# A two-layer decoder trunk on one core: w_gate and w_up both by seven products in another order, four slots for weight parts and 52 general tiles

## The chip, the cores and the metric

The kernel runs on one core of one Trainium2 chip. The metric is device time in microseconds of one execution, as the median over runs. Its engines are PE (TensorE: matmuls and transposes), PEld (TensorE's weight loads, which run beside PE), DVE (VectorE), ACT (ScalarE), POOL (GpSimd) and SP (SyncE, which issues the DMAs). [...] A difference of 0.2% is about what a measurement of this kernel can tell from no change.

## What is computed

```python
S, D, DEPTH, HID = 512, 1024, 2, 2816          # tokens, model width, layers, FFN width
for layer in range(DEPTH):
    h = h + hybrid_mixer(rmsnorm(h, norm_mix[layer]), w_in[layer], ...)    # attention + Mamba-2, one projection in, one out
    h = h + swiglu(rmsnorm(h, norm_ffn[layer]), w_gate[layer], w_up[layer], w_down[layer])
return rmsnorm(h, final_norm)

def swiglu(h, w_gate, w_up, w_down):            # w_gate, w_up: 1024 x 2816; w_down: 2816 x 1024
    return (silu(h @ w_gate) * (h @ w_up)) @ w_down
```

Everything is float32. The change touches how `h @ w_gate` and `h @ w_up` are made, how much room two pools have, and the first instructions of the program.

## The kernel before

**Layout.** Activations are kept transposed: a tile is 128 features by 512 tokens (2 KB a partition), and `hT` is eight such tiles. A float32 operand is split in two parts, `hi` (the value cast to the faster float32r form) and `lo` (the rest), and each product of two tiles is three matmuls: hi by hi, hi by lo, lo by hi. Of a weight of 128 rows by 128 columns PE loads 128x128 and streams the tokens past it.

**A plan sets the order.** The program first records every operation (`plan.add` with an engine, a cost, its outputs and inputs), each with a due time (`at(...)` and `clock[0]`, which counts PE work). `Plan.schedule` then runs through them as a list scheduler would: each engine takes the ready operation with the smallest due time for which its tiles have room. What comes out is a fixed order for every engine; each engine then works through its own queue strictly in that order and waits where an input or a buffer is missing. SP's loads are taken in the order of their due times alone. Numbers such as the tiles of a pool therefore change the order of everything.

**Pools.** `G(...)` takes a tile of 128x512 from the general pool `g` (`NG` tiles); `whi` and `wlo` hold the two parts of a weight piece of up to eight 128x128 blocks (`NWH` slots each, 4 KB a partition); `raw` holds a weight chunk of 1 MB as it lands (two slots); `big` holds the sums `wsum` (two slots). PSUM has three banks `acc`, two `hold` and three `tr`. `split_w` makes the two parts: ACT casts `raw` to `whi`, DVE subtracts to make `wlo`.

**FFN.** The 22 column tiles of `w_gate` and `w_up` are taken in four parts, `PARTS` = 6, 6, 6, 4. A part takes its tiles in pairs of 256 columns: first `w_gate`, then `w_up`, then SiLU and the product, then the part's rows of `w_down`. Part 0 makes both directly. Parts 1 to 3 make `w_gate` directly: two `block`s of 8 row blocks x 3 = 24 matmuls of 512 columns each, so 48. They make `w_up` by `seven`: the 256 columns, the 1024 rows and the 512 tokens are each cut in two, and the 2x2x2 block product is made with seven products of half size instead of eight (Winograd's form of Strassen). A product is 4 row blocks x 3 = 12 matmuls of 256 tokens, so 84 in all. It needs three weight pieces of eight blocks, called here a (raw columns), b and c (sums of raw blocks), and one of four, d; DVE makes four sums of 128x512 and the parts `wlo`, ACT makes the parts `whi`. The activations' sums (`X`, by `normed`) are made once a layer. In PSUM the products end in `p17`, `p26`, `p45` and `p3`; ACT copies the first, `e`, and five DVE additions make the two column tiles `m` and `o`.

**Start.** SP issues `pmix` (scales), then by turns `hT[k]` and the first weights `raw0[k]` (256 KB each). PE works at once on nine products of `ones`; then, for each k, ACT and DVE split both tiles and PE runs 12 matmuls of 512 columns on them (the first four column tiles of `w_in`). `norm_next.square` squares `hT[k]` on ACT for the first norm.

Of the kernel before, what the change touches and what calls it, by code (L numbers as in the profile page):

```python
# [14 lines left out]
AF = mybir.ActivationFunctionType  # L15
ALU = mybir.AluOpType
# [3 lines left out]
P = 128  # L20
S = 512
# [6 lines left out]
NH = 16  # L28
HID = 2816
NRAW = 2  # L30
NWH = 3
NG = 56
LEAD = 14.0
KTOK = 4
TABLE_COST = 10.0
# [5 lines left out]
E_XW = 'dve'  # L41
RES_G = 6
NEAR_G = 6.0
GATE7 = 0
PARTS = (6, 6, 6, 4)
HH = S // 2
KQ = KD // 2
# [132 lines left out]
class VTile:  # L180


    def __init__(self, pool, shape, dtype, tag, name, space):
        self.pool, self.shape, self.dtype, self.tag, self.name = pool, shape, dtype, tag, name
        self.psum = space
        self.ap = None
        self.writer, self.readers, self.uses = None, [], 0
        self.live = False

    def get(self):  # L190
        if self.ap is None:
# [12 lines left out]
class Plan:  # L204
# [4 lines left out]
    def add(self, eng, dur, outs, ins, fn, prio=None, table=None, lat=0.0):  # L209
        o = Op()  # L210
        o.eng, o.dur, o.lat, o.fn, o.table = eng, dur, lat, fn, table
        o.prio = self.t if prio is None else prio
        o.n, o.users = len(self.ops), []
        deps = set()
        outs = [v.tile for v in outs]
        ins = [v.tile for v in ins if isinstance(v, View)]
        for t in ins:
            assert t.writer is not None, f"{t.name} is read before it is written"
            deps.add(t.writer)
        for t in outs:  # L220
            if t.writer is not None:
                deps.add(t.writer)
            deps.update(t.readers)
        for t in ins:
            t.readers.append(o)
        for t in outs:
            t.writer, t.readers = o, []
        deps.discard(o)
        o.tiles = list({id(t): t for t in outs + ins}.values())
        for t in o.tiles:  # L230
            t.uses += 1
        o.deps = deps
        for d in deps:
            d.users.append(o)
        self.ops.append(o)
        return o
# [107 lines left out]
def hybrid_trunk(  # L344
# [40 lines left out]
    def hold():  # L385
        return new(ps, [P, S], F32, ("hold", 2), "hold", True)
# [39 lines left out]
    def memset(eng, o, val):  # L426
        plan.add(eng, 0.1 + 0.9e-3 * o.free, [o], [], lambda: ENG[eng].memset(R(o), val))

    TABLE = {AF.Exp: "exp", AF.Ln: "ln", AF.Silu: "silu", AF.Sin: "silu"}

    def act(o, a, func, scale=None, bias=None, accum=None):
        ptr = [s for s in (scale, bias) if isinstance(s, View)]
        outs = [o] + ([accum] if accum is not None else [])

        def fn():
            kw = {}
            if scale is not None:
                kw["scale"] = R(scale)
            if bias is not None:
                kw["bias"] = R(bias)  # L440
            if accum is not None:
                kw["accum_out"] = R(accum)
            if func == AF.Copy and not kw:
                nc.scalar.copy(R(o), R(a))  # L444
            else:
                nc.scalar.activation(R(o), R(a), func, **kw)  # L446
        cost = 0.83e-3 * o.free + (0.053 if a.tile.psum else 0.093) + 0.093 * len(ptr)
        plan.add("act", cost, outs, [a] + ptr, fn, table=TABLE.get(func))

    def mms(outs, prods, each, prio=None):  # L450

# [7 lines left out]
                    nc.tensor.matmul(R(p[0]), R(p[1]), R(p[2]), start=p[3], stop=p[4])  # L459
        plan.add("pe", each * len(prods), outs, ins, fn, prio, lat=0.08)  # L460

    def load(o, src, kb):
        plan.add("sp", max(0.47, kb / 351.0), [o], [], lambda: nc.sync.dma_start(R(o), src), lat=2.0)

    def tposes(t, parts, name=None):
        mms([t], parts, 0.108)


    at(-40.0)
    pmix = C([P, 16], "pmix")  # L470
    load(pmix, columns[:, PC_MIX:PC_MIX + 16], 8)
    hT = [C([P, S], f"hT{k}") for k in range(KD)]

    raw0 = []
    for k in range(KD):
        load(hT[k], xT[k * P:(k + 1) * P, :], 256)
        raw0.append(G("w0"))
        load(raw0[k], w_in[0, k * P:(k + 1) * P, XBC_COL + 1024:XBC_COL + 1024 + S], 256)
    at(-35.0)
    ones = C([P, P], "ones")  # L480
    memset("pool", ones, 1.0)

    t = tr()
    mms([t], [(t[:, 0:P], ones, ones, True, True)] * 9, 0.43)
    nhalf = C([P, NT], "nhalf")
    memset("pool", nhalf, -0.5)

# [63 lines left out]
    class Norm:  # L551
# [2 lines left out]
        def __init__(self, n):  # L554
            self.n, self.ss, self.row = n, None, None

        def square(self, tl, eng="dve"):
            s = G("sq")
            act(s, tl, AF.Square)
            if self.ss is None:  # L560
                self.ss = s
            else:
                tt(eng, self.ss, self.ss, s, ALU.add)
# [31 lines left out]
    for k in range(KD):  # L595
        at(-20.0 + k)
        xs_next.append(split_x(hT[k], pmix[:, k:k + 1]))
        wh, wl = split_x(raw0[k], None)
        for j, t in enumerate(first):
            js = slice(j * P, (j + 1) * P)  # L600
            xh, xl = xs_next[k]
            mms([t], [(t, wh[:, js], xh, k == 0, False), (t, wh[:, js], xl, False, False),
                      (t, wl[:, js], xh, False, k == KD - 1)], 0.2165, clock[0])
            clock[0] += 3 * 0.2165
        at(-12.0 + k)
        norm_next.square(hT[k])


    at(-12.0)
# [504 lines left out]
    def seven(ids, X):  # L1114
        raw = whl[ids[0]][0]
        q = [[raw[:, j * KQ:(j + 1) * KQ, i * P:(i + 1) * P] for j in range(2)] for i in range(2)]
        at(clock[0] - LEAD)

        def split(src, nk=KD):
            hi, lo = new(wp, [P, 8, P], F32R, ("whi", NWH), "whi"), new(wp, [P, 8, P], F32R, ("wlo", NWH), "wlo")  # L1120
            copy("act", hi[:, 0:nk, :], src)
            tt("dve", lo[:, 0:nk, :], src, hi[:, 0:nk, :].bitcast(F32), ALU.subtract)
            return hi, lo
        a = split(raw[:, :, 0:P])
        sm = big("wsum").rearrange("p (k c) -> p k c", c=P)
        s = [sm[:, i * KQ:(i + 1) * KQ, :] for i in range(4)]
        tt("dve", s[0], q[1][0], q[1][1], ALU.add)
        tt("dve", s[1], s[0], q[0][0], ALU.add)
        tt("dve", s[2], q[0][0], q[1][0], ALU.add)
        tt("dve", s[3], q[0][1], s[1], ALU.add)  # L1130
        b = split(sm[:, 0:KD, :])
        c = split(sm[:, KD:, :])
        d = split(q[1][1], KQ)
        t1_, t2_ = slice(0, HH), slice(HH, S)

        def prod(o, w, k0, xs, half):
            hi, lo = w
# [12 lines left out]

        def halves(v):
            return v.rearrange("p (u c) -> p u c", u=2)

        b1, b2 = X["b"][0:KQ], X["b"][KQ:]
        p17, p26 = hold(), acc()
        e, m, o = G("e"), G("m"), G("o")
        prod(p17[:, 0:HH], a, 0, b1, t1_)
        copy("act", e[:, 0:HH], p17[:, 0:HH])
        prod(p26[:, 0:HH], a, KQ, b2, t1_)
        prod(p26[:, HH:], b, KQ, X["t12"], t2_)  # L1160
        tt("dve", halves(m), halves(p26), bcast(e[:, 0:HH]), ALU.add)
        p45, p3 = acc(), tr()
        prod(p45[:, HH:], b, 0, X["t12"], t1_)
        prod(p17[:, HH:], c, 0, X["t34"], t1_)
        tt("dve", e[:, HH:], p17[:, HH:], m[:, HH:], ALU.add)
        prod(p3[:, 0:HH], c, KQ, b2, t2_)
        tt("dve", m[:, HH:], m[:, HH:], p3[:, 0:HH], ALU.add)
        tt("dve", m[:, HH:], m[:, HH:], p45[:, HH:], ALU.add)
        prod(p45[:, 0:HH], d, 0, X["t34"], t2_)
        tt("dve", halves(o), halves(p45), bcast(e[:, HH:]), ALU.add)  # L1170
        at(clock[0] - 4.0)
        return m, o

# [100 lines left out]
```

## Time and profile before

| | |
|---|---|
| median of 3 runs | 1323.34 us (1321.87 to 1323.98) |
| the profiled execution | 1324.0 us, of which the span from first to last instruction is 1322.2 us |
| PE busy | 1294.6 us (98%), 6674 matmuls |
| DVE busy | 905.7 us (68%) |
| ACT busy | 653.0 us (49%) |
| POOL busy | 140.2 us (11%) |
| DMA | 115.57 MB, mean 87 GB/s |
| granted clock of TensorE, mean | 0.995 |

Busy is the union of an engine's instructions. A matmul's end is modelled and overlaps the next one's start, so what PE takes for a matmul is read from start to start in the timeline, not from its duration. The same holds for DVE, whose instructions also overlap by some 0.1 us.

### The profile page before, as it was taken

What the parts mean: (1) busy time and instruction counts of PE and PEld (TensorE: products, weight loads), DVE (VectorE), ACT (ScalarE), POOL (GpSimd) and SP (SyncE); (2) the same over time, 40 slices, a digit from 0 to 9 for tenths busy, and PEclk for the clock granted to TensorE, in tenths of its full rate; (3) what the DMA queues carried; (4) which work ended last, traced back from release to release, by engine and by line L of the source; (5) the groups of instructions that cost most, each with busy time, mean ns of one, the idle gap of its engine ahead of it and who ended that gap; (6) DMA issues with size and microseconds to landing.
All of it is one profiled execution on the core that took longest, in us unless ns stands there. A gap on an engine that the chain in (4) does not pass through costs nothing.

```text
span 1322.2 us, 17020 instructions
## 1 busy us (share of the span) xinstructions
PE 1294.6 (98%) x6674; PEld 1067.4 (81%) x6674; DVE 905.7 (68%) x1510; ACT 653.0 (49%) x1029; POOL 140.2 (11%) x109
## 2 busy tenths in 40 slices
PE   8999998999999999999999999999999999999997
PEld 7877776778888888888888777767888889888896
DVE  6987779768746555555779687887786456465464
ACT  7677656656323323323647687466553233243253
POOL 0014455000000000000000234620000000000000
PEclk9999999999999999999999999999999999999999
DMA  7222211123232233233332222111332332322421
GB/s 242 64 64 64 64 65 64 33 80 102 90 112 96 69 123 99 78 112 96 96 98 65 94 66 65 56 40 45 88 112 84 119 96 72 120 96 73 135 96 63
DMA packets 105727, 115.57 MB, mean 87 GB/s; under 512 B 4656, under 2 KB 95024, under 8 KB 105648
## 3 DMA queue, kind: packets, MB, share of 16 engines
q1 hardware_dynamic: 105648, 114.49, 27.4%
q8 instruction: 52, 0.85, 0.3%
q14 instruction: 27, 0.22, 0.1%
HBM read 112.39 MB, written 2.10 MB: 87 GB/s over the span
## 4 chain that ended last, share of the span: by engine, by line
PE 87%; DVE 7%; ACT 2%; POOL 2%; issue 1%; DMA 0%; POOLq 0%; SPq 0%; DVEq 0%; ACTq 0%
PE acc L459 72%; PE hold L459 7%; PE tr L459 6%; PE tr L457 3%; DVE wlo L407 2%; DVE qs L407 1%; POOL xbc L407 1%; DVE xbc L418 1%; POOL qr L407 1%; ACT whi L444 1%; DVE wsum L407 0%; DVE qs L921 0%; POOL qs L407 0%; ACT L446 0%; DVE sa L413 0%
## 5 line engine op out<-in xcount | busy, mean ns | idle before, releaser
L459 PE MATMUL acc<-xh,whi 128*128 128x512 f32 (+1 forms) x1552 | 588.4, 379 | 1.4 <-DVE o L407 0.9
L459 PE MATMUL acc<-xl,whi 128*128 128x512 f32 (+1 forms) x1552 | 579.4, 373 | 0.0
L459 PE MATMUL acc<-xh,wlo 128*128 128x512 f32 (+1 forms) x1536 | 573.3, 373 | 4.2 <-DVE wlo L407 4.2
L444 ACT CAST whi<-raw 128x1024 fp32r<-128x1024 f32 (+3 forms) x248 | 212.4, 859 | 335.2 <-PE acc L459 303.0
L459 PEld LDWEIGHTS acc<-xh,whi 128*128 128x128 f32 x1552 | 293.2, 189 | 55.1 <-issue 5.6
L459 PEld LDWEIGHTS acc<-xh,wlo 128*128 128x128 f32 x1536 | 289.7, 189 | 58.6 <-DVE wlo L407 6.7
L459 PEld LDWEIGHTS acc<-xl,whi 128*128 128x128 f32 x1552 | 293.3, 189 | 47.1 <-issue 0.5
L407 DVE TENSOR_TENSOR wlo<-raw,whi 128x1024 fp32r<-128x1024 f32 (+2 forms) x240 | 246.8, 1030 | 27.6 <-ACT whi L444 27.3
L407 DVE TENSOR_TENSOR hT<-hT,acc 128x512 f32<-128x512 f32 x104 | 71.1, 685 | 103.6 <-PE acc L459 102.9
L407 DVE TENSOR_TENSOR wlo<-wsum,whi 128x1024 fp32r<-128x1024 f32 x32 | 39.0, 1224 | 88.4 <-ACT whi L444 88.4
L573 POOL TENSOR_TENSOR rcol<-var,nhalf 128x4 f32<-128x4 f32 x8 | 8.7, 1089 | 577.2 <-DVE var L413 577.2
L446 ACT ACT_TABLE_LOAD x49 | 62.9, 1283 | 6.6 <-DMA hT<-in_xT_dram 4.1
L444 ACT CAST whi<-wsum 128x1024 fp32r<-128x1024 f32 x32 | 33.5, 1048 | 53.9 <-PE acc L459 46.3
L418 DVE SCALAR_TENSOR_TENSOR xbc<-cu,prm,xbc 128x511 f32<-128x511 f32 (+2 forms) x72 | 58.4, 819 | 0.8
L444 ACT CAST xh<-ga 128x512 fp32r<-128x512 f32 x44 | 27.3, 621 | 54.5 <-DVE ga L407 38.6
L446 ACT ACTIVATE sa<-sa,mx 128x512 f32<-128x512 f32 (+3 forms) x64 | 36.0, 562 | 36.5 <-DVE mx L979 36.2
L1230 POOL TENSOR_TENSOR fr<-fvar,nhalf 128x1 f32<-128x1 f32 x4 | 2.2, 546 | 353.5 <-DVE fvar L413 353.5
L979 DVE CUSTOM_DVE_ANT_0 sa<-tr,cst 128x512 f32<-128x512 f32 (+3 forms) x64 | 30.7, 479 | 10.3 <-PE tr L459 10.2
L459 PE MATMUL hold<-xh,wlo 128*128 128x256 f32 x128 | 36.3, 284 | 0.0
L459 PE MATMUL hold<-xl,whi 128*128 128x256 f32 x128 | 36.2, 283 | 0.0
L459 PE MATMUL hold<-xh,whi 128*128 128x256 f32 x128 | 36.1, 282 | 0.0
L407 DVE TENSOR_TENSOR xl<-ga,xh 128x512 fp32r<-128x512 f32 x44 | 30.3, 688 | 8.3 <-ACT xh L444 8.2
(216 smaller groups left out, 1654.8 us busy)
## 6 DMA issues: line engine op xcount, KB each, us to landing
raw<-in_w_in_dram SPq DMA_DIRECT2D x24, 1024.0 KB, 5.1
raw<-in_w_gate_dram SPq DMA_DIRECT2D x22, 1024.0 KB, 5.2
raw<-in_w_up_dram SPq DMA_DIRECT2D x22, 1024.0 KB, 5.2
raw<-in_w_down_dram SPq DMA_DIRECT2D x24, 768.0 KB, 4.5
raw<-in_w_out_dram SPq DMA_DIRECT2D x8, 1024.0 KB, 5.0
raw<-in_w_out_dram SPq DMA_DIRECT2D x8, 512.0 KB, 6.3
hT<-in_xT_dram SPq DMA_DIRECT2D x8, 256.0 KB, 5.3
w<-in_w_in_dram SPq DMA_DIRECT2D x8, 256.0 KB, 5.4
```

Source lines behind the costliest of these rows:

```text
L407: lambda: ENG[eng].tensor_tensor(R(o), R(a), R(b), alu))
L418: lambda: nc.vector.scalar_tensor_tensor(R(o), R(a), R(s), R(b), op0, op1))
L444: nc.scalar.copy(R(o), R(a))
L446: nc.scalar.activation(R(o), R(a), func, **kw)
L457: nc.tensor.transpose(R(p[0]), R(p[1]), R(p[2]))
L459: nc.tensor.matmul(R(p[0]), R(p[1]), R(p[2]), start=p[3], stop=p[4])
L573: lambda: nc.gpsimd.tensor_tensor(R(self.r), R(v), R(nhalf), ALU.pow))
L979: nc.vector.tensor_tensor_reduce(R(sa[:, 0:nk]), R(t[:, 0:nk]), R(cst[:, C_MASK + S - nk:C_MASK + S]), 1.0, 3e38, ALU.add, ALU.min, R(m))
L1230: lambda r=r, v=v: nc.gpsimd.tensor_tensor(R(r), R(v), R(nhalf[:, 0:1]), ALU.pow))
```

## The change

`GATE7` becomes 1: in parts 1 to 3 of both layers `w_gate` is made by `seven` too (8 pairs a layer, 16 in all). `seven` takes its steps in another order: d is split first after a, b's sums and parts come before c's, d's product moves from the seventh place to the third, and the two additions that read `p45` are asked for earlier. To let b be split before the other two sums exist, a view of part of a tile can stand as a tile of its own for the order (`Part`). `NWH` goes from 3 to 4 and `NG` from 56 to 52, so the SBUF taken stays the same. At the start `ones` is set first, `hT[0]` is loaded ahead of `pmix`, the first weights are issued from ACT's queue, one small activation stands ahead of the first real one, `ones` has ten products, and the squares are held back behind later splits. `hT`'s adds, `w_down`, the mixer and part 0 are as they were, but their order is planned anew.

```diff
-NWH = 3
-NG = 56
+NWH = 4
+NG = 52
-GATE7 = 0
+GATE7 = 1
...
-    load(pmix, columns[:, PC_MIX:PC_MIX + 16], 8)
...
         load(hT[k], xT[k * P:(k + 1) * P, :], 256)
+        if k == 0:
+            load(pmix, columns[:, PC_MIX:PC_MIX + 16], 8)
         raw0.append(G("w0"))
-        load(raw0[k], w_in[0, k * P:(k + 1) * P, XBC_COL + 1024:XBC_COL + 1024 + S], 256)
+        load(raw0[k], w_in[0, k * P:(k + 1) * P, XBC_COL + 1024:XBC_COL + 1024 + S], 256, "sp" if k else "act")
+
+    warm = small([P, 1], "warm", 1)
+    act(warm, ones[:, 0:1], AF.Square)
...
-    mms([t], [(t[:, 0:P], ones, ones, True, True)] * 9, 0.43)
+    mms([t], [(t[:, 0:P], ones, ones, True, True)] * 10, 0.43)
...
+    for k in range(KD):
         at(-12.0 + k)
-        norm_next.square(hT[k])
+        norm_next.square(hT[k], after=[xs_next[min(k + 3, KD - 1)][0]])
...
         a = split(raw[:, :, 0:P])
+        d = split(q[1][1], KQ)
         sm = big("wsum").rearrange("p (k c) -> p k c", c=P)
-        s = [sm[:, i * KQ:(i + 1) * KQ, :] for i in range(4)]
+        sums = [part(sm[:, 0:KD, :]), part(sm[:, KD:, :])]
+        s = [sums[i // 2][:, i % 2 * KQ:(i % 2 + 1) * KQ, :] for i in range(4)]
         tt("dve", s[0], q[1][0], q[1][1], ALU.add)
         tt("dve", s[1], s[0], q[0][0], ALU.add)
+        b = split(sums[0])
         tt("dve", s[2], q[0][0], q[1][0], ALU.add)
         tt("dve", s[3], q[0][1], s[1], ALU.add)
-        b = split(sm[:, 0:KD, :])
-        c = split(sm[:, KD:, :])
-        d = split(q[1][1], KQ)
+        c = split(sums[1])
...
-        p17, p26 = hold(), acc()
+        p17, p26, p45, p3 = hold(), acc(), acc(), tr()
...
         prod(p26[:, 0:HH], a, KQ, b2, t1_)
+        prod(p45[:, 0:HH], d, 0, X["t34"], t2_)
         prod(p26[:, HH:], b, KQ, X["t12"], t2_)
         tt("dve", halves(m), halves(p26), bcast(e[:, 0:HH]), ALU.add)
-        p45, p3 = acc(), tr()
         prod(p45[:, HH:], b, 0, X["t12"], t1_)
         prod(p17[:, HH:], c, 0, X["t34"], t1_)
         tt("dve", e[:, HH:], p17[:, HH:], m[:, HH:], ALU.add)
+        tt("dve", halves(o), halves(p45), bcast(e[:, HH:]), ALU.add)
+        tt("dve", m[:, HH:], m[:, HH:], p45[:, HH:], ALU.add)
         prod(p3[:, 0:HH], c, KQ, b2, t2_)
         tt("dve", m[:, HH:], m[:, HH:], p3[:, 0:HH], ALU.add)
-        tt("dve", m[:, HH:], m[:, HH:], p45[:, HH:], ALU.add)
-        prod(p45[:, 0:HH], d, 0, X["t34"], t2_)
-        tt("dve", halves(o), halves(p45), bcast(e[:, HH:]), ALU.add)
```

At the very start of ACT's queue stood this before (`w` is the first weights' tile, `xh` the hi part of it or of `hT`, `sq` a square):

```order
1 L446 ACT_TABLE_LOAD
2 L446 ACTIVATE xh_102<-hT_2_90,pmix_72 128x512
3 L446 ACTIVATE sq_106<-hT_2_90 128x512
4 L444 CAST xh_112<-w_10_92 128x512
5 L446 ACTIVATE xh_116<-hT_3_98,pmix_72 128x512
6 L444 CAST xh_120<-w_11_100 128x512
7 L446 ACTIVATE sq_130<-hT_3_98 128x512
```

Now there stands this:

```order
1 L480 DMA w_11_76<-in_w_in_dram 128x512
2 L463 ACT_TABLE_LOAD
3 L463 ACTIVATE warm_95<-ones_72 128x1
4 L461 CAST xh_107<-w_11_76 128x512
5 L463 ACTIVATE xh_109<-hT_3_74,pmix_93 128x512
6 L463 ACTIVATE xh_115<-hT_4_97,pmix_93 128x512
7 L461 CAST xh_123<-w_12_103 128x512
```

The first weights are issued here, the table load no longer stands behind a tile of `hT`, and the first square has moved from the third place to the eleventh.

DVE's queue in layer 0's part 1, where the weights of the second pair are made ready, held this before: the four sums of a seven, the parts a, d, b and c of `w_up`, and the end of the first pair (`o`, `ga`, `xl`) between them:

```order
579 L407 TENSOR_TENSOR wsum_3773<-raw_3701 128x512
580 L407 TENSOR_TENSOR wsum_3773<-wsum_3773,raw_3701 128x512
581 L407 TENSOR_TENSOR o_3790<-acc_3668,e_3657 128x512
582 L407 TENSOR_TENSOR wsum_3773<-raw_3701 128x512
583 L418 SCALAR_TENSOR_TENSOR ga_3675<-o_3790,ga_3675 128x512
584 L407 TENSOR_TENSOR wlo_3801<-raw_3701,whi_3788 128x1024
585 L407 TENSOR_TENSOR xl_3811<-ga_3675,xh_3803 128x512
586 L407 TENSOR_TENSOR wsum_3773<-raw_3701,wsum_3773 128x512
587 L407 TENSOR_TENSOR wlo_3824<-raw_3701,whi_3820 128x512
588 L407 TENSOR_TENSOR wlo_3872<-wsum_3773,whi_3862 128x1024
589 L407 TENSOR_TENSOR wlo_3882<-wsum_3773,whi_3874 128x1024
```

Now the seven of the second pair's `w_gate` is made ready there, among the additions that end the first pair's `w_up` (`m_3797`, `e_3743`, `o_3836`):

```order
580 L424 TENSOR_TENSOR wsum_3745<-raw_3565 128x512 x2
581 L424 TENSOR_TENSOR wsum_3745<-wsum_3745,raw_3565 128x512
582 L424 TENSOR_TENSOR wlo_3764<-raw_3565,whi_3754 128x1024
583 L424 TENSOR_TENSOR wsum_3745<-raw_3565,wsum_3745 128x512
584 L424 TENSOR_TENSOR wlo_3787<-raw_3565,whi_3778 128x512
585 L424 TENSOR_TENSOR m_3797<-acc_3719,e_3743 128x512
586 L424 TENSOR_TENSOR e_3743<-hold_3709,m_3797 128x256
587 L424 TENSOR_TENSOR wlo_3821<-wsum_3745,whi_3811 128x1024
588 L424 TENSOR_TENSOR o_3836<-acc_3747,e_3743 128x512
589 L424 TENSOR_TENSOR m_3797<-m_3797,acc_3747 128x256
590 L435 SCALAR_TENSOR_TENSOR o_3707<-o_3836,o_3707 128x512
591 L424 TENSOR_TENSOR m_3797<-m_3797,tr_3813 128x256
```

A `w_gate` piece thus costs DVE a seven's rows where it had two `wlo` of 128x1024, and the parts of one seven are made while the one before it is still on PE.

## Rows read from the trace of the kernel before

**Rows 1.** The page: span, busy time of PE and DVE, chain that ended last

```profile
span 1322.2 us, 17020 instructions
PE 1294.6 (98%) x6674; PEld 1067.4 (81%) x6674; DVE 905.7 (68%) x1510; ACT 653.0 (49%) x1029; POOL 140.2 (11%) x109
...
PE 87%; DVE 7%; ACT 2%; POOL 2%; issue 1%; DMA 0%; POOLq 0%; SPq 0%; DVEq 0%; ACTq 0%
```

**Rows 2.** Windows: from one part's FFN to the same place of the next

```profile
core 0: us, PE busy (x) PEld busy (x) DVE busy (x) ACT busy (x) POOL busy (x), PEclk, DMA share, GB/s
...
507.37:604.40 97.03, 96.40 (x541) 84.13 (x540) 55.25 (x74) 32.00 (x42) 0.00 (x0) 1.00 0.30 98
1159.27:1256.60 97.33, 96.14 (x542) 84.23 (x540) 55.19 (x74) 32.01 (x42) 0.00 (x0) 1.00 0.33 103
```

**Rows 3.** Timeline of PE: start, duration, operation; w_gate (397 us) and a seven (441 us)

```profile
398.17 0.39 PE L459 MATMUL acc<-xh,wlo 128*128 128x512 f32 x1
398.40 0.39 PE L459 MATMUL acc<-xh,whi 128*128 128x512 f32 x1
...
441.00 0.28 PE L459 MATMUL hold<-xl,whi 128*128 128x256 f32 x1
441.12 0.28 PE L459 MATMUL hold<-xh,wlo 128*128 128x256 f32 x1
```

**Rows 4.** Groups by shape: busy us, mean ns of one, idle before

```profile
L407 DVE TENSOR_TENSOR wlo<-raw,whi 128x1024 fp32r<-128x1024 f32 x120 | 149.7, 1250 | 16.5 <-ACT whi L444 16.2
...
L407 DVE TENSOR_TENSOR wsum<-raw 128x512 f32<-128x512 f32 x32 | 22.0, 687 | 14.8 <-DMA raw<-in_w_up_dram 14.7
```

**Rows 5.** Timeline of DVE in layer 0, part 1: start, duration, operation

```profile
418.83 0.42 DVE L407 TENSOR_TENSOR e<-hold,m 128x256 f32<-128x256 f32 x1
419.17 1.22 DVE L407 TENSOR_TENSOR wlo<-raw,whi 128x1024 fp32r<-128x1024 f32 x1
420.30 0.41 DVE L407 TENSOR_TENSOR m<-m,tr 128x256 f32<-128x256 f32 x1
420.75 0.42 DVE L407 TENSOR_TENSOR m<-m,acc 128x256 f32<-128x256 f32 x1
421.21 0.69 DVE L407 TENSOR_TENSOR ga<-ga,m 128x512 f32<-128x512 f32 x1
421.81 1.22 DVE L407 TENSOR_TENSOR wlo<-raw,whi 128x1024 fp32r<-128x1024 f32 x1
```

**Rows 6.** Waits: engine, line, waited for; us in total, times, longest

```profile
ACT whi L444 <- PE acc L459: 349.2, 178, 6.0
...
PE acc L459 <- DVE wlo L407: 4.2, 5, 1.3
```

**Rows 7.** Timeline of the program's start, all engines

```profile
1.18 0.42 SPq L463 DMA_DIRECT2D hT<-in_xT_dram  x1
1.64 0.42 SPq L463 DMA_DIRECT2D w<-in_w_in_dram  x1
...
4.11 1.28 ACT L446 ACT_TABLE_LOAD   x1 [4.11 <-DMA hT<-in_xT_dram]
...
5.41 0.72 ACT L446 ACTIVATE xh<-hT,pmix 128x512 fp32r<-128x512 f32 x1
...
6.56 0.60 ACT L444 CAST xh<-w 128x512 fp32r<-128x512 f32 x1
...
7.21 0.57 PE L459 MATMUL acc<-xh,xh 128*128 128x512 f32 x1 [2.49 <-ACT xh L444]
...
30.74 0.95 PE L459 MATMUL tr<-ones,sq 128*128 128x1 f32 x8
```

**Rows 8.** Windows of the start: us, PE busy, granted clock, DMA share, GB/s

```profile
4.00:5.00 1.00, 0.72 (x6) 1.00 0.88 299
5.00:7.00 2.00, 0.00 (x0) 1.00 0.96 348
...
8.00:10.00 2.00, 2.00 (x6) 0.50 1.01 381
```

More of the change, by code (lines that the diff above doesn't have):

```diff
@@ L186, in __init__ @@
         self.ap = None
+        self.root = self
         self.writer, self.readers, self.uses = None, [], 0
@@ L194, in get, with __init__, part @@
         return self.ap
+class Part:
+    def __init__(self, view):
+        self.view, self.root = view, view.tile
+        self.pool, self.tag, self.name, self.psum = None, None, view.tile.name, view.tile.psum
+        self.writer, self.readers = None, []
+    def get(self):
+        return self.view.real()
+def part(view):
+    return View(Part(view), view.shape)
 class Op:
@@ L228, in add @@
         deps.discard(o)
-        o.tiles = list({id(t): t for t in outs + ins}.values())
+        o.tiles = list({id(t.root): t.root for t in outs + ins}.values())
         for t in o.tiles:
@@ L429, in hybrid_trunk, with act @@
     TABLE = {AF.Exp: "exp", AF.Ln: "ln", AF.Silu: "silu", AF.Sin: "silu"}
-    def act(o, a, func, scale=None, bias=None, accum=None):
+    def act(o, a, func, scale=None, bias=None, accum=None, after=()):
         ptr = [s for s in (scale, bias) if isinstance(s, View)]
@@ L447, in act @@
         cost = 0.83e-3 * o.free + (0.053 if a.tile.psum else 0.093) + 0.093 * len(ptr)
-        plan.add("act", cost, outs, [a] + ptr, fn, table=TABLE.get(func))
+        plan.add("act", cost, outs, [a] + ptr + list(after), fn, table=TABLE.get(func))
     def mms(outs, prods, each, prio=None):
@@ L460, in mms, with load @@
         plan.add("pe", each * len(prods), outs, ins, fn, prio, lat=0.08)
-    def load(o, src, kb):
-        plan.add("sp", max(0.47, kb / 351.0), [o], [], lambda: nc.sync.dma_start(R(o), src), lat=2.0)
+    def load(o, src, kb, eng="sp"):
+        plan.add(eng, max(0.47, kb / 351.0), [o], [], lambda: ENG[eng].dma_start(R(o), src), lat=2.0)
     def tposes(t, parts, name=None):
@@ L469, in hybrid_trunk @@
     at(-40.0)
+    ones = C([P, P], "ones")
+    memset("pool", ones, 1.0)
     pmix = C([P, 16], "pmix")
-    load(pmix, columns[:, PC_MIX:PC_MIX + 16], 8)
     hT = [C([P, S], f"hT{k}") for k in range(KD)]
@@ L476, in hybrid_trunk @@
         load(hT[k], xT[k * P:(k + 1) * P, :], 256)
+        if k == 0:
+            load(pmix, columns[:, PC_MIX:PC_MIX + 16], 8)
         raw0.append(G("w0"))
-        load(raw0[k], w_in[0, k * P:(k + 1) * P, XBC_COL + 1024:XBC_COL + 1024 + S], 256)
+        load(raw0[k], w_in[0, k * P:(k + 1) * P, XBC_COL + 1024:XBC_COL + 1024 + S], 256, "sp" if k else "act")
+    warm = small([P, 1], "warm", 1)
+    act(warm, ones[:, 0:1], AF.Square)
     at(-35.0)
-    ones = C([P, P], "ones")
-    memset("pool", ones, 1.0)
     t = tr()
-    mms([t], [(t[:, 0:P], ones, ones, True, True)] * 9, 0.43)
+    mms([t], [(t[:, 0:P], ones, ones, True, True)] * 10, 0.43)
     nhalf = C([P, NT], "nhalf")
@@ L555, in __init__, with square @@
             self.n, self.ss, self.row = n, None, None
-        def square(self, tl, eng="dve"):
+        def square(self, tl, eng="dve", after=()):
             s = G("sq")
-            act(s, tl, AF.Square)
+            act(s, tl, AF.Square, after=after)
             if self.ss is None:
```

## Prediction

> **What bounds the kernel now.** I start with the page. PE is busy for 98% of the span of 1322.2 us, and 87% of the chain that ended last is PE's [rows 1]; DVE has 68%. A matmul's busy time is modelled, so the first question is whether PE runs at its pace or waits. For that I take a stretch of the FFN that repeats: from the first product of a part's `w_up` to the same place one part later is 97.03 us in layer 0 and 97.33 in layer 1 [rows 2]. The timeline of PE gives the pace there: a matmul of 512 columns starts 0.227 us after the one before it, one of 256 columns 0.120 us after [rows 3]. A full part has three pairs: 3 x 48 matmuls of `w_gate`, 3 x 84 of `w_up`, and 144 of `w_down`. That is 288 x 0.227 + 252 x 0.120 = 65.3 + 30.2 = 95.5 us. So of 97.0 to 97.3 us only some 1.5 to 1.8 are lost, and the clock is 1.00 throughout [rows 2]. The FFN is bound by the number and size of its matmuls. DVE has 55.2 of the 97 us there, so it is far from full over a whole part; whether it is so inside the pairs is the question below. The start is another matter: PE's first matmul on real data comes at 7.21 us, after 2.49 us of waiting for ACT [rows 7].
>
> **w_gate by seven products.** Removed per pair: 48 x 0.227 = 10.88 us of PE. Added: 84 x 0.120 = 10.08 us. That is 0.80 us less, though the columns streamed fall by an eighth: the pace of 256 columns is more than half of that of 512. There are 8 pairs a layer and 2 layers, so 16 x 0.80 = 12.8 us less, all on PE and on the path.
>
> The Trainium skill's page "TensorE: Matmul & The Clock Gate", section "Back-to-back issue gap", gives N / 2.4 GHz + 2.5 ns for one matmul after another, so 216 ns and 109 ns; by this a pair would win 10.36 - 9.17 = 1.19 us and the sum would be 19.1 us. The same section says that with weight loads between the matmuls both set the spacing. The rows show 227 and 120 with a weight load for each matmul; I go by the rows.
>
> **What DVE has to do for it.** Per `w_gate` piece it made two `wlo` of 128x1024. A seven wants three of these, one of 128x512 (d), four sums of 128x512, and afterwards two additions of 512 and three of 256 elements. By the mean durations (1.25 us for 1024, 0.69 for 512 [rows 4], 0.42 for 256 [rows 5]) that is 3.75 + 0.69 + 2.75 + 1.38 + 1.26 = 9.8 us in place of 2.5. A pair, with two sevens and four more operations of 0.69 (the two products, the two `xl`), comes to 22.4 us of durations, where PE needs 2 x 10.08 = 20.16. By durations DVE would be the slower engine inside the pairs. But the timeline shows that its instructions overlap: after the 1.22 us `wlo` at 419.17 the next one starts 1.13 us later, after the 512-element one at 421.21 0.60 later, after the 256-element one at 418.83 0.34 later, and 0.45 later where the next reads its result [rows 5]. From start to start a seven is 3 x 1.13 + 7 x 0.60 + 0.34 + 2 x 0.45 = 8.83 us, and a pair 17.7 + 2.4 = 20.1 us. So DVE's pace is just PE's, nearly full for the 60 us of a part's pairs, and whatever it waits for makes it late.
>
> What covers that is how far ahead it works. In the planned order DVE's a and d of the next seven stand ahead of `m`, which waits for the fourth product of the seven that is on PE (the fifth runs interleaved with it); so they can be ready two products early, 2 x 12 x 0.120 = 2.9 us, and b follows `m` closely and is first read three products later than a, some 4.3 us more. During `w_down` (144 x 0.227 = 32.7 us of PE) DVE has only eight `wlo` of 768 elements and eight additions, under 8 x 1.25 + 8 x 0.69 = 15.5 us, and works ahead on the first seven of the next part. If the cover is gone, the price is DVE's pace in place of PE's, as in the first rival. ACT gains two casts' worth and a copy a piece and stays near half: 32.0 us of 97 now [rows 2].
>
> **Four slots, 52 tiles, the new order in a seven.** ACT waits for PE to free a slot for 349 us in total before it casts a `whi`, but PE itself waits only 4.2 us for a `wlo` [rows 6]. A fourth slot lets each part be made one product earlier; in the FFN it can give back at most the loss found above, 1.5 to 1.8 us a part, for six parts some 10 us. A seven needs four parts, so I expect the slot to be used up by the second seven, and the nearly full DVE to eat what it gives: I put the two together at 0, between -8 (nearly all of the loss gone) and +8 (it doubles). The order of d's product costs PE nothing, since the products are the same. The four general tiles fewer are missed only where the pool is full, which in the planned order is around part 0's end, when `X` is made, and at the program's end. There PE has some 30 us of direct products in hand before `X` is read. I put it at 0; the upper bound is one `wlo` a place, 4 x 1.25 = 5 us. The mixer's queues are planned anew with these numbers, with neighbours swapped on DVE, PE and POOL; nothing in them is longer, so 0, between -3 and +3 (a wait like that of 4.2 us coming or going).
>
> **The start.** `hT[0]` was issued at 1.18 us, one step of 0.46 behind `pmix`, and ACT began at 4.11 when it had landed, with a table load of 1.28 us; then came one split, a square and the weights' cast, and PE started at 7.21 [rows 7]. Now the table load lies in the wait. `hT[0]` should land at about 4.11 - 0.46 = 3.65. The first weights come through ACT's queue at the same time; the two share what the DMA moves, 299 GB/s in that stretch [rows 8], so the later of the two 256 KB may be 0.88 us behind, at 4.5. With 0.60 us for the cast and 0.72 for the split [rows 7], PE starts between 5.0 and 5.8; I take 5.4, which is 1.8 us earlier. The second thing is the clock: it was full until PE went idle, and the first real matmuls ran at the lower level, 0.50 between 8 and 10 us [rows 8]. With ten products of `ones` (nine ended by 4.72 [rows 8]) the idle time nearly vanishes; if the clock then stays at 2.4 GHz, at least half of these 2 us comes back, 1.0. Together 2.8 us, between 1.2 (the clock falls all the same, the weights land late) and 3.8. After it PE runs without a gap to 30.74 [rows 7], and what comes next hangs on PE's sum of squares, so the gain is carried on if ACT and DVE have the squares summed by then, which with their work begun earlier I take for granted.
>
> The Trainium skill's entry page "Trainium Kernel Development and Optimization" says that DMAs from several queues run on the same 16 engines, so that a second queue saves issue time alone. By that the weights gain 0.46 to 0.9 us of issuing and no transfer time, which is inside the bounds above.
>
> **Sum.** 1324.0 - 12.8 - 2.8 = 1308.4 us for an execution like the profiled one. That one stands 0.7 above the median of 1323.3, so I predict 1308.
>
> **Rivals.**
> First, DVE becomes the bound in the pairs. If each of its instructions had to end before the next began, or if waits for ACT and PE cost it as much, a pair would take 22.4 us in place of 10.88 + 10.08 = 20.96: 16 x 1.44 = 23 us more, with the start's 2.8 off 1344 us. It is on the slower side from about 21.1 us of DVE a pair (20.96 + 2.8/16). The Trainium skill's page "VectorE: DVE Perf Modes", section "The DRAIN you can't avoid", has such a rule: the next operation does not start until the pipe is empty. Against it are the starts of 1.13 and 0.60 above, and the head start. I give the full case, slower, 0.05, and a case in the middle that leaves no measurable difference (a pair near 21) 0.07.
>
> Second, DVE's waits eat only part of the gain: the loss a part rises from 1.6 to about 3, and the start brings 1.5. 1324 - 12.8 - 1.5 + 8 = 1318; 0.22 for 1313 to 1320.
>
> Third, more than forecast: the slot removes most of the FFN's losses (-8) with the start at 2.8, 1300; or the pace of 256 columns comes down to what the page gives, 6 us more, 1302. Nothing in the rows speaks for the pace; for the slot there are the 349 us of waiting. 0.14 for under 1303.
>
> Fourth, the start does nothing because the norm or DVE is the real limit after 31 us: 1311. It lies inside the forecast's own range, 1303 to 1313, which has 0.52.
>
> **Numbers.** About 0.2%, 2.6 us, is what a measurement of this kernel can tell. Faster: 0.52 + 0.22 + 0.14 = 0.88; same 0.07; slower 0.05. The range leaves out the two last and the edge of the third: 1300 to 1318.
>
> **What would show it.** In the profile after: PE matmuls up by 576 (16 x 36) and two for `ones`; the first real matmul near 5.4 us at clock 1.00; a part from one `w_up` to the next at 97.0 - 2.4 = 94.6 us; DVE near 77 us of it (55.2 + 3 x 7.3), and nearly full in the pairs. I am wrong if PE's waits for `wlo`, `m` or `o` grow to more than a microsecond a pair, or if the mixer's stretches between the FFNs change by more than 3 us.

## The result, and the profile after

| | before | after |
|---|---|---|
| median of four runs each | 1323.66 us (1321.87 to 1326.15) | 1303.2 us (1300.53 to 1304.99) |
| the profiled execution, its span | 1324.0, 1322.2 | 1300.5, 1298.7 |
| start to PE's first sum of squares | 30.74 | 28.29 |
| FFN of layer 0: first product on `ath` (the mixer's out projection, just ahead of the FFN) to the next norm's sum of squares | 391.2 | 380.6 |
| FFN of layer 1: the same place to the end | 392.4 | 382.0 |
| the rest (both mixers) | 507.8 | 507.9 |

The ratio is 0.984 [0.981, 0.986], 20.5 us less. The time lies in the predicted range, 5 us below the predicted 1308. Three executions in the experiments' sets that took over 1.5% longer than the quickest of the same kernel are left out of ratios and medians. The profiled execution of after is the quickest of its four runs; its span is 23.5 us shorter, and 21.0 of that is in the two FFNs, which further kernels with the same FFN repeat within 0.3 us. I therefore compare FFNs by those two stretches, called the FFN sum: 783.6 us before, 762.6 after. An FFN sum comes from the one profiled execution of a kernel.

The page of after, its lines for [rows 1]: span, busy time and instructions of each engine, and the chain that ended last.

```profile
span 1298.7 us, 18535 instructions
...
PE 1278.3 (98%) x7252; PEld 1083.8 (83%) x7252; DVE 1002.7 (77%) x1686; ACT 692.3 (53%) x1086; POOL 143.2 (11%) x109
...
PE 88%; DVE 6%; ACT 2%; POOL 2%; issue 1%; DMA 1%; POOLq 0%; DVEq 0%
```

There are 578 more matmuls in 16 us less of busy PE, and DVE has 97 us more; the chain is PE's as before. Windows of after answer to [rows 2]: the three pairs of one part, then a whole part in layer 0 and one in layer 1.

```profile
core 0: us, PE busy (x) PEld busy (x) DVE busy (x) ACT busy (x) POOL busy (x), PEclk, DMA share, GB/s
399.27:419.46 20.19, 20.19 (x170) 20.19 (x169) 17.73 (x25) 9.14 (x12) 0.00 (x0) 1.00 0.32 97
419.46:439.60 20.14, 20.14 (x171) 20.14 (x170) 19.87 (x31) 10.23 (x14) 0.00 (x0) 1.00 0.23 71
439.60:459.80 20.20, 20.20 (x165) 19.94 (x164) 17.70 (x28) 9.96 (x14) 0.00 (x0) 1.00 0.32 99
...
488.99:582.44 93.45, 93.45 (x650) 87.42 (x648) 72.92 (x107) 37.51 (x50) 0.00 (x0) 1.00 0.32 102
1129.70:1222.90 93.20, 93.20 (x650) 87.50 (x649) 72.60 (x107) 37.48 (x50) 0.00 (x0) 1.00 0.32 102
```

Two things are to be seen. A part takes 93.2 to 93.5 us where 97.0 was, and I had forecast 94.6. Its matmuls alone, 504 x 0.120 + 144 x 0.227 = 93.2 us at the pitches of [rows 3], fill it; the 1.5 to 1.8 us that a part lost are gone. And DVE has 19.87 of the 20.14 us of the middle pair, as full as worked out, but 17.7 in the first and the third, 55.3 of 60.5 over the three; PE hardly ever waits for it. PE's waits in layer 0's FFN (397 to 660 us; engine, line, waited for, total, times, longest) were three groups with 3.0 us before:

```profile
PE acc L459 <- DVE wlo L407: 1.7, 3, 0.6
PE acc L459 <- DVE o L407: 0.9, 1, 0.9
PE acc L459 <- DVE m L407: 0.4, 1, 0.4
```

After has half a microsecond:

```profile
PE acc L476 <- ACT xh L461: 0.3, 1, 0.3
PE acc L476 <- DVE xl L424: 0.2, 1, 0.2
```

The timeline of after's start answers to [rows 7]:

```profile
0.73 0.41 ACTq L480 DMA_DIRECT2D w<-in_w_in_dram  x1
...
0.73 0.38 SPq L480 DMA_DIRECT2D hT<-in_xT_dram  x1
...
1.17 1.28 ACT L463 ACT_TABLE_LOAD   x1 [1.17 <-PEq L1279]
...
4.49 0.62 ACT L461 CAST xh<-w 128x512 fp32r<-128x512 f32 x1 [1.82 <-DMA w<-in_w_in_dram]
...
5.02 1.33 ACT L463 ACTIVATE xh<-hT,pmix 128x512 fp32r<-128x512 f32 x2
...
5.79 0.50 PE L476 MATMUL acc<-xh,xh 128*128 128x512 f32 x1 [0.16 <-ACT xh L463]
```

Both loads go out at 0.73, the table load is over before they land, and PE starts at 5.79 in place of 7.21. The weights land at 4.49, the late end of what I had allowed.

### The profile page after: what moved, and what is told of

Read it like the earlier page. It is cut to its first block, busy times and chain, and to the rows that moved or that the text cites. A ratio compares the mean times of both kernels' runs of the same rounds, so it can differ in the third digit from the quotient of the medians.

```text
span 1298.7 us, 18535 instructions
## 1 busy us (share of the span) xinstructions
PE 1278.3 (98%) x7252; PEld 1083.8 (83%) x7252; DVE 1002.7 (77%) x1686; ACT 692.3 (53%) x1086; POOL 143.2 (11%) x109
## 4 chain that ended last, share of the span: by engine, by line
PE 88%; DVE 6%; ACT 2%; POOL 2%; issue 1%; DMA 1%; POOLq 0%; DVEq 0%
PE acc L476 67%; PE hold L476 10%; PE tr L476 8%; PE tr L474 3%; DVE wlo L424 1%; DVE qs L424 1%; DVE xbc L435 1%; DVE ee L424 1%; POOL qs L424 0%; DMA raw<-in_w_in_dram 0%; ACT xh L463 0%; POOL qr L424 0%; ACT kh L461 0%; POOL rcol L594 0%; DVE qs L943 0%
## 5 line engine op out<-in xcount | busy, mean ns | idle before, releaser
L476 PE MATMUL acc<-xh,wlo 128*128 128x512 f32 (+1 forms) x1536 | 545.2, 355 | 0.0
L461 ACT CAST whi<-wsum 128x1024 fp32r<-128x1024 f32 x64 | 67.2, 1050 | 114.0 <-PE acc L476 62.8
L424 DVE TENSOR_TENSOR wlo<-wsum,whi 128x1024 fp32r<-128x1024 f32 x64 | 78.0, 1220 | 4.2 <-ACT whi L461 4.2
L476 PE MATMUL hold<-xh,wlo 128*128 128x256 f32 x256 | 72.4, 283 | 0.0
L476 PE MATMUL hold<-xl,whi 128*128 128x256 f32 x256 | 72.4, 283 | 0.0
L476 PE MATMUL hold<-xh,whi 128*128 128x256 f32 x256 | 72.4, 283 | 0.0
L424 DVE TENSOR_TENSOR wsum<-raw 128x512 f32<-128x512 f32 x64 | 41.8, 687 | 26.8 <-DMA raw<-in_w_gate_dram 19.3
L476 PEld LDWEIGHTS hold<-xh,whi 128*128 128x128 f32 x256 | 49.1, 192 | 0.5
L476 PEld LDWEIGHTS hold<-xl,whi 128*128 128x128 f32 x256 | 49.1, 192 | 0.5
L476 PEld LDWEIGHTS hold<-xh,wlo 128*128 128x128 f32 x256 | 49.1, 192 | 0.0
```

The costliest lines, as they stand in the source:

```text
L424: lambda: ENG[eng].tensor_tensor(R(o), R(a), R(b), alu))
```

## The experiments

Each was timed beside runs of before on the same chip. Ratios are to those. The runs fall in three such sets, in which before has medians of 1324.3, 1326.7 and 1325.4, so kernels of different sets are compared by their ratios or FFN sums.

**The three parts of the FFN's change, one at a time, and the change without its fourth slot.** `g7_alone` is before with one number changed:

```diff
-GATE7 = 0
+GATE7 = 1
```

> Only GATE7 = 1 on the kernel before: three slots, 56 tiles, the old order in a seven, the old start. The sum says 12.8 us less of matmuls. The changed kernel shows 8 us more in the FFN, because PE's waits there are gone. Slot theory (the fourth slot took the waits away): they stay here or grow, so about 1311 (-12.8 us). Order theory (the new order in a seven took them away): the same, about 1311. Kind theory (they stood at the joint between direct w_gate and the seven, and go when both are sevens): about 1303 (-20 us). A full part lasts 94.6 us by the first two, 93.1 by the third.

`slots_alone` is before with the pools changed:

```diff
-NWH = 3
-NG = 56
+NWH = 4
+NG = 52
```

> Only four slots and 52 tiles on the kernel before. Slot theory: PE's waits in the FFN go, about 1316 (-8 us), a full part lasts 95.5 us. Order theory and kind theory: the part stays at 97 us and the time at 1324, give or take 3 us of the mixer's new order.

`order_alone` is before with the new `seven` and `Part`, as in the change's diff from `class Part` and in `seven`, so for `w_up` only:

```diff
+        d = split(q[1][1], KQ)
...
+        b = split(sums[0])
...
+        prod(p45[:, 0:HH], d, 0, X["t34"], t2_)
         prod(p26[:, HH:], b, KQ, X["t12"], t2_)
```

> Only the new order in a seven on the kernel before, for w_up. Order theory: PE's waits in the FFN go, about 1316 (-8 us), a full part lasts 95.5 us. Slot theory and kind theory: 97 us and 1324.

`after_three_slots` is after with the pools of before:

```diff
-NWH = 4
-NG = 52
+NWH = 3
+NG = 56
```

> The changed kernel with three slots and 56 tiles again. Slot theory: the waits come back, 8 us or more, so 1311 or above, and a part of 94.6 us or more. Order theory and kind theory: as the changed kernel, 1303, and a part of 93.2 us.

| kernel | median | ratio to before | FFN sum, to before |
|---|---|---|---|
| `g7_alone` | 1325.9 | 1.002 [1.000, 1.003] | 784.3, +0.7 |
| `slots_alone` | 1319.7 | 0.996 [0.995, 0.997] | 778.3, -5.3 |
| `order_alone` | 1319.2 | 0.995 [0.993, 0.997] | 775.4, -8.3 |
| `after_three_slots` | 1306.3 | 0.986 [0.984, 0.987] | 762.8, -20.8 |

The parts do not add, and none of the three theories had expected 1326 for `g7_alone`. `w_gate` by sevens has 12.8 us less work for PE and wins nothing by itself. Its waits of PE in layer 0's FFN:

```profile
PE acc L459 <- DVE m L407: 5.6, 5, 1.1
PE acc L459 <- DVE wlo L407: 3.0, 5, 0.6
PE acc L459 <- DVE o L407: 0.9, 1, 0.9
```

That is 9.5 us where before had 3.0, so the 6.4 us won in this layer are spent on waits for `m` (which frees a bank) and for weight parts. Near the end of layer 1 the clock falls as well, in the window:

```profile
core 0: us, PE busy (x) PEld busy (x) DVE busy (x) ACT busy (x) POOL busy (x), PEclk, DMA share, GB/s
...
1276.00:1300.00 24.00, 20.61 (x136) 19.22 (x135) 13.76 (x23) 11.26 (x19) 0.00 (x0) 0.86 0.20 69
```

This profiled execution, 1329.9 us, is one of four that took 1328 to 1330; the other five took 1324.6 to 1325.9, and whether the clock falls there in them too, no trace shows.

The order by itself removes 8.3 us without any `w_gate` in sevens, and with the order in place `w_gate` brings 775.4 - 762.8 = 12.6 us. The fourth slot wins 5.3 us alone and 0.2 on top of the order. Both remove the waits for `wlo` and `m` in layer 0; the slot leaves one for `o`, first line, and the order, second line, almost nothing:

```profile
PE acc L459 <- DVE o L407: 1.4, 1, 1.4
PE acc L476 <- DVE xl L424: 0.2, 1, 0.2
```

Counted from start to start against the pitches of [rows 3], PE's waits in before's two FFNs cost 6.6 us and slower matmuls 2.7 more; in `order_alone` these are 0.5 and 1.3. By whole times `slots_alone` and `order_alone` are alike, so that the order is worth 3 us more than the slot is shown by one profile of each alone; with `w_gate` in sevens whole times show it too (0.993 for `g7_slots`, next, against 0.986 for `after_three_slots`, which has the new start besides). Medians carry what the mixers did in each run besides (last section), so that 1306.3 and 1303.2 do not contradict 762.8 and 762.6.

**Sevens with the slots, without the order; the start alone.** `g7_slots`:

```diff
-NWH = 3
-NG = 56
+NWH = 4
+NG = 52
...
-GATE7 = 0
+GATE7 = 1
```

> Both weights by sevens, four slots and 52 tiles, but the old order in a seven and the old start. Slot theory (a fourth slot alone lets the sevens run without waits): the waits of 0.76 us for wlo and 1.3 us for m that both-by-sevens with three slots showed in every pair of layer 0 go, a full part lasts 93.1 us, the time is about 1306. Order theory (the banks that the old order holds until d's product, the last, make PE wait for m whatever the slots): the waits for m stay, 16 x 1.3 us at most, a part lasts 95 to 97 us, about 1312 to 1320.

It ran in 1315.7 us, 0.993 [0.991, 0.994]; FFN sum 771.5, -12.1, which is 8.9 more than after. PE's waits in layer 0's FFN are 3.2 us:

```profile
PE acc L459 <- DVE wlo L407: 2.0, 2, 1.0
PE acc L459 <- DVE o L407: 0.9, 1, 0.9
...
```

So the slots repair much of what `g7_alone` suffers, but not all: with them `w_gate` by sevens is worth 778.3 - 771.5 = 6.8 us. `start_alone` is before with all lines of the change outside `seven` and the three constants:

```diff
+        load(raw0[k], w_in[0, k * P:(k + 1) * P, XBC_COL + 1024:XBC_COL + 1024 + S], 256, "sp" if k else "act")
...
+    act(warm, ones[:, 0:1], AF.Square)
...
+        norm_next.square(hT[k], after=[xs_next[min(k + 3, KD - 1)][0]])
```

> Only the new start on the kernel before (GATE7 = 0, three slots, 56 tiles, the old order in a seven). Start theory: the first real matmul near 5.8 us as in the changed kernel, the sum of squares of the first norm 2 us earlier, carried to the end: 1321.5 (-2 us, -0.15%). Rival: DVE or the norm's chain after 31 us swallows it, 1324.

It ran in 1323.5, 0.998 [0.997, 0.999], which is 3.1 us less than the 1326.7 beside it; the FFN sum is 783.8, unchanged. PE's first real matmul came at 5.89 us and the first sum of squares at 30.08, as against 28.29 in after and 30.74 in before; the last section shows why. This one profile thus has 0.7 us of the 3.1 at the start. Where the rest of the median's gain lies is not shown; it may be the mixers' scatter.

**Is DVE really full?** `dve_plus4` puts four additions per seven on DVE that nobody reads:

```diff
         c = split(sums[1])
+        for _ in range(4):
+            x = G("extra")
+            tt("dve", x, X["b"][0][0].bitcast(F32), X["b"][1][0].bitcast(F32), ALU.add)
```

> The changed kernel with four more additions of 128x512 on DVE in every seven, whose results nobody reads: 8 x 0.60 = 4.8 us of DVE a pair more from start to start. Pace theory (DVE is full at 20.1 of 20.16 us a pair and has some 7 us of head start a part): a pair then wants 24.9 us, a part of three is late by 14.4 - 7 = 7 us, one of two by 2 to 3 us, in sum 30 to 40 us, so about 1335. Rival (DVE still has room, its busy share of a whole part being 78%, and w_down's stretch takes it): under 8 us more, 1303 to 1311.

It ran in 1301.7, 0.983 [0.981, 0.985], with the FFN sum of after, 762.9. This told nothing: the additions depend on `X` alone, so the plan put all 128 between 374 and 1193 us where DVE was free. `dve_tied4` makes them of the seven's own sums (again nobody reads them):

```diff
+        for _ in range(4):
+            x = G("extra")
+            tt("dve", x.rearrange("p (k c) -> p k c", c=P), s[0], s[2], ALU.add)
```

> The changed kernel with four more additions of 128x512 on DVE in every seven, this time of the seven's own sums, so that they can't be done early; nobody reads their results. Pace theory (in the pairs DVE is full at 20.1 of 20.16 us, with some 7 us of head start a part): a pair wants 24.9 us of DVE, a full part is late by 14.4 - 7 = 7 us, one of two pairs by 2 to 3, in sum 30 to 40 us: 1333 to 1343. Rival (DVE has room all the same): under 8 us more.

It ran in 1317.3, 0.994 [0.992, 0.996], FFN sum 778.3: 15.7 more than after, 15.2 of it in layer 0 and 0.5 in layer 1. Its windows: the stretch of after's middle pair and the next part in layer 0, then a part of layer 1.

```profile
core 0: us, PE busy (x) PEld busy (x) DVE busy (x) ACT busy (x) POOL busy (x), PEclk, DMA share, GB/s
419.46:439.60 20.14, 20.14 (x168) 19.99 (x168) 20.12 (x32) 8.71 (x12) 0.00 (x0) 1.00 0.32 104
489.00:583.00 94.00, 88.14 (x615) 82.73 (x615) 80.55 (x122) 35.74 (x48) 0.00 (x0) 0.98 0.29 91
...
1146.00:1240.00 94.00, 94.00 (x654) 88.10 (x653) 86.92 (x132) 38.11 (x50) 0.00 (x0) 1.00 0.34 104
```

And PE's waits in layer 0:

```profile
PE acc L476 <- DVE m L424: 4.9, 3, 2.9
PE acc L476 <- ACT whi L461: 2.7, 3, 1.4
PE acc L476 <- DVE wlo L424: 1.9, 2, 1.2
...
```

In layer 0 DVE has no room left and PE waits: over the three pairs from 499 to 560 us DVE is busy for 60.9 of 61.0 us and PE for 55.1. In layer 1 the same additions fit: 86.9 us of DVE in 94, spread over the pairs and `w_down`, and PE never waits, though DVE has 59.7 of the 60.0 us from 1150 to 1210. A full DVE inside the pairs is therefore not yet a bound. That what DVE has done ahead, under `w_down`, covers it in layer 1 and runs out in layer 0 fits this, but was not tested. The result lies between the two theories; which detail of the two layers' plans decides was not tried.

**Which piece of the order.** `d_last` is after with d split last, its product last and `p45` read last, as in before:

```diff
-        d = split(q[1][1], KQ)
...
         c = split(sums[1])
+        d = split(q[1][1], KQ)
...
-        prod(p45[:, 0:HH], d, 0, X["t34"], t2_)
...
+        prod(p45[:, 0:HH], d, 0, X["t34"], t2_)
+        tt("dve", halves(o), halves(p45), bcast(e[:, HH:]), ALU.add)
```

> The changed kernel, with d's part split last, d's product last and p45 read last again, as before; b is still split ahead of c's sums. Bank theory (d's early product, with the early reads of p45, frees the bank that the next seven waits for): the waits for m and o come back, 16 x 0.5 to 1.3 us, about 1311 to 1316. Sum theory (b's early split is what took the waits away): as the changed kernel, 1303.

`b_late` is after with b split only when all four sums are there:

```diff
-        b = split(sums[0])
...
-        c = split(sums[1])
+        b = split(sm[:, 0:KD, :])
+        c = split(sm[:, KD:, :])
```

> The changed kernel, with b split only after all four sums as before; d's product stays third. Bank theory: as the changed kernel, 1303, the waits stay away. Sum theory: waits for wlo come back, 16 x 0.7 us, about 1311.

`d_last` ran in 1310.7, 0.988 [0.986, 0.990], FFN sum 770.2, 7.6 more than after: most of what the whole order is worth there (`g7_slots`: 8.9). Layer 0 has 380.9 as after; layer 1 alone loses. Its PE timeline at the last part:

```profile
1261.06 0.28 PE L476 MATMUL acc<-xh,wlo 128*128 128x256 f32 x1
1262.54 0.39 PE L476 MATMUL hold<-xh,whi 128*128 128x256 f32 x1 [1.20 <-ACT whi L461]
1262.76 0.28 PE L476 MATMUL hold<-xl,whi 128*128 128x256 f32 x1
1263.87 0.39 PE L476 MATMUL hold<-xh,wlo 128*128 128x256 f32 x1 [0.83 <-DVE wlo L424]
...
1265.13 0.41 PE L476 MATMUL acc<-xh,wlo 128*128 128x256 f32 x1
1265.34 0.41 PE L476 MATMUL hold<-xh,whi 128*128 128x256 f32 x1
```

A wait for `whi` and one for `wlo`, and 1.3 us after the second PE goes on at the lower level of the clock, 0.21 us from one matmul of 256 columns to the next in place of 0.12, until 1268.3. Two waits for `m` (1.9 us) stand ahead of these, at 1052 and 1248 us. Counted from start to start against the pitches of [rows 3], the four waits cost 4.6 us, half of it in the two for `m`, and slower matmuls 2.3 us more than after has in this layer: 6.9 of its 7.3. `b_late` ran in 1303.3, 0.982 [0.980, 0.985], FFN sum 762.4: as after. So with d's product third the early b, and with it `Part`, is worth nothing measurable. Without d's place the early b is enough in layer 0, where `g7_slots` has 384.1 and `d_last` 380.9, but not in layer 1, where they have 387.4 and 389.3. Of the two pieces d's place (its part split early, its product third, `p45` read early) is enough alone; it was not taken apart further.

**More sevens.** If PE's matmuls are all that is left in the FFN, the pairs of part 0 should move into parts with sevens. `parts_4666` is after with

```diff
-PARTS = (6, 6, 6, 4)
+PARTS = (4, 6, 6, 6)
```

> The changed kernel with the FFN cut into parts of 4, 6, 6, 6 tiles in place of 6, 6, 6, 4: one pair a layer moves from the direct part to the sevens, 2 x 2 x 0.80 = 3.2 us of matmuls less in both layers (w_gate and w_up of the pair). If X is ready in time after four tiles and the program's end bears a part of two pieces of w_down more: 1300 (-0.25%). Rival: part 1 waits for X or the end gets longer, 1303 or above.

and `parts_2668` has

```diff
-PARTS = (6, 6, 6, 4)
+PARTS = (2, 6, 6, 8)
```

> The changed kernel with the FFN in parts of 2, 6, 6, 8 tiles: one pair a layer more by sevens than with 4, 6, 6, 6, so 3.2 us less once more: 1294 if X is ready in time. Rival: part 0 with 21.8 us of direct products and 10.9 us of w_down is too short for DVE to make X (some 20 us) beside its own work, PE waits at part 1, 1297 or above.

`parts_4666` ran in 1297.1, 0.979 [0.977, 0.980]: faster than both kernels. Its FFN sum is 757.0, 5.6 less than after, where the two pairs more (one a layer) would give 2 x (96 x 0.227 - 168 x 0.120) = 3.3. Of the rest 1.4 is no gain: layer 0's stretch has six matmuls of 512 columns fewer than the pair accounts for, since the plan moved them behind the sum of squares that ends it. Another 0.5 is the waits that after has in layer 0 and this kernel has not. `parts_2668` ran in 1333.1, 1.005 [1.003, 1.007]. One window ahead of part 1 in layer 0, and PE's waits from 300 us to 1290:

```profile
core 0: us, PE busy (x) PEld busy (x) DVE busy (x) ACT busy (x) POOL busy (x), PEclk, DMA share, GB/s
...
330.00:340.00 10.00, 1.24 (x2) 0.79 (x3) 8.69 (x18) 3.60 (x6) 0.00 (x0) 0.50 0.00 1
...
```

```profile
PE acc L476 <- ACT xh L461: 28.7, 2, 14.4
```

Part 0's direct products are the cover under which DVE makes `X`. With two tiles there PE stands twice for 14.4 us until `X` is ready.

## Why the prediction was right, and where its size was off

**w_gate by seven products, -12.8.** Right in size: 12.6 us between `order_alone` and `after_three_slots`, with 578 more matmuls as counted. The pitches of 0.227 and 0.120 us, with a weight load for each matmul, held. The estimate of 19.1 us (16 x 1.19 is 19.0), worked out from a formula on the Trainium skill's page "TensorE: Matmul & The Clock Gate", section "Back-to-back issue gap", did not come; that section gives the formula for the isolated matmul.

**Four slots, 52 tiles, the new order in a seven, 0.** This is the step that was mis-sized: it was worth some -8.5 us (-8.3 by the order alone, 0.2 more with the slot), at the lower of the bounds that I had given it. The sum gave 1308.4 for an execution like the profiled one, and after's took 1300.5; these 7.9 us are this term, less 0.6 by which the two others fell short. That the median lies only 5 us off the forecast is after's scatter: its other three executions took 1302.9 to 1305.0. I had written that the order of d's product "costs PE nothing, since the products are the same" and looked for the gain in the slot only. `order_alone` has the whole 8.3 with three slots, the slot adds 0.2 to it, `b_late` shows that the early b can be left out, and `d_last` that d's place cannot. In the code, d's product needs no sums and stands between a's products and b's, and `p45` is read before the seven ends; whether the later need of b or the earlier release of the bank does it was not taken apart. `d_last` has waits of both kinds.

My reason for the 0, that a nearly full DVE would eat what the slot gives, was half right. DVE is full in a part's middle pair, 19.87 of 20.14 us, and `dve_tied4` shows the price beyond that in layer 0. But the other two pairs have 17.7, and over a part it had 72.9 us of 93.45. I had forecast 77, by adding durations, though busy time counts an overlap once; by the starts that I had read a pair wants 6.6 us more, and the part 75. The prediction also missed that its two terms hang on each other: -12.8 comes only together with the order; with the slots alone it is -6.8, without order and slots +0.7.

**The start, -2.8.** 2.45 us between the two profiles to the first sum of squares, 3.1 in the medians of `start_alone` with 0.7 in its profile. PE's first matmul came at 5.79, not 5.4, since the weights landed late. The full clock that I had counted on for 1.0 us came in after and in five of the other eight kernels with the new start, which reach the first sum of squares at 28.3 to 28.5 us; in three it did not, and they come there at 30.0 to 30.1, where before came at 30.74. Nor was the clock full until PE went idle, as I had read from the granted clock of [rows 8]: by spacing, before's products of `ones` (two equal records each) stand 0.213 us apart until 4.1 us and only the last few 0.111, and after's stand 0.213 apart to their end at 5.2. So in after the full clock did not stay but came, with the first real matmuls. The term has two outcomes rather than one, and the old start scatters too: 29.3 to 31.8 in five profiles, 30.8 on average, against 28.9 with the new one. By these averages the term is -1.9, inside its bounds of 1.2 to 3.8 but smaller than I had it, and that the two profiled executions came so near to 2.8 is partly luck. Where the clock stayed full in both, 29.26 in `slots_alone` and 28.29 in after, the earlier start brings 1.0 of the 1.8 that I had given it; after's second matmul waits for DVE's split, 0.28 us. The rows are in the last section.

**The mixer and 52 tiles, 0.** 507.8 and 507.9 us in the two profiles agree with it, though mixers scatter by more than that from profile to profile (last section).

**The rivals.** DVE as the bound did not occur. If each instruction had waited for the end of the one before, a pair would take 22.4 us; after's DVE timeline has starts 0.60 us apart at durations of 0.68. The Trainium skill's page "VectorE: DVE Perf Modes", section "The DRAIN you can't avoid", has the rule of the empty pipe and adds that a next operation that is not held starts earlier; the trace agrees with the addition, which the prediction left out:

```profile
425.60 0.68 DVE L424 TENSOR_TENSOR wsum<-raw,wsum 128x512 f32<-128x512 f32 x1
426.21 0.68 DVE L424 TENSOR_TENSOR m<-m,m 128x512 f32<-128x512 f32 x1
426.81 0.68 DVE L424 TENSOR_TENSOR xl<-o,xh 128x512 fp32r<-128x512 f32 x1
```

The second rival, waits that eat part of the gain, is what `g7_alone` and `g7_slots` did, and the order took it away. The third, more than forecast, had the size of what happened (its 1300 is the profiled execution's time, at the edge of the range) but named the slot as its cause.

## What to carry to other kernels

Parts of a change that each look free can be the condition for the part that saves work: cost the saved work and the waits it creates together, and test them both ways round, each alone and each left out. In a chain of products, ask first which operand needs no sums and put its product between the ones whose operands are being made, and read the bank that it fills early; with that a fourth buffer brought only 0.2 us more. An engine that is full in one stage need not be the bound: in layer 1 of `dve_tied4` a DVE busy for 59.7 of 60.0 us held nobody up.

## What the hardware showed that was not expected

After PE has waited, its clock falls for a while in some profiles and not in others, with the same instructions ahead of it. At the start of `start_alone` and of after, whose starts are the same in the code, PE's timeline reads, first `start_alone`, then after:

```profile
5.89 0.80 PE L476 MATMUL acc<-xh,xh 128*128 128x512 f32 x1 [0.26 <-ACT xh L463]
6.68 0.80 PE L476 MATMUL acc<-xl,xh 128*128 128x512 f32 x1
...
8.12 0.63 PE L476 MATMUL acc<-xl,xh 128*128 128x512 f32 x1
8.55 0.63 PE L476 MATMUL acc<-xh,xl 128*128 128x512 f32 x1
```

```profile
7.39 0.40 PE L476 MATMUL acc<-xl,xh 128*128 128x512 f32 x1
7.63 0.40 PE L476 MATMUL acc<-xh,xl 128*128 128x512 f32 x1
```

Matmuls of 512 columns stand 0.43 us apart in the one, for seven of them, and 0.23 in the other; 7 x 0.20 = 1.4 us, a slower one on either side of them (0.25 and 0.08 us) and a start 0.10 us later make the 1.8 us between 30.08 and 28.29. With the new start six of nine profiles have none at 0.43 and three have seven; with the old start four of five have 5 to 13, and one has none. What decides I don't know. The record of the granted clock misses this at the start: the window of `start_alone` from 8 to 10 us says 1.00 at the pitch of 0.43, that of before 0.50 [rows 8]. The spacing of equal matmuls is the safer reading.

The same happens in the mixers, and there it makes scatter. At the second norm of the first one, around 205 to 220 us, PE waits for POOL, DVE and ACT in every run. Windows of PE alone, `slots_alone` first, then `g7_slots`, whose code is the same there:

```profile
core 0: us, PE busy (x), PEclk, DMA share, GB/s
...
215.00:220.00 5.00, 4.71 (x13) 0.50 0.00 0
220.00:225.00 5.00, 5.00 (x23) 0.93 0.02 4
```

```profile
215.00:220.00 5.00, 4.10 (x21) 1.00 0.00 0
220.00:225.00 5.00, 5.00 (x26) 1.00 0.02 5
```

The first mixer, from the first sum of squares to `ath`, took 251.5 us in the one and 247.7 in the other, and 246.9 to 252.9 over all profiles, while equal FFNs agreed within 0.3. Set side by side matmul by matmul from the first sum of squares on, the two are level at 210 us (in `slots_alone`), 3.8 us apart at 223.5, and still so at `ath`; these windows make the difference between the two. The like would account for medians of after and of `after_three_slots` that lie 3 us apart at the same FFN sum, and the mean granted clock of their runs, 0.993 to 0.996 and 0.989 to 0.992, fits it; no trace of those other runs shows it.
